# Attention score products issued in pairs, their steps spread over fewer gate units, and three loads re-cut, in a two-layer hybrid trunk on one core

## The chip, the cores and the metric

One Trainium2 chip, one of its cores. The metric is the device time of one execution in microseconds, the median over repeated executions of the same program.

## The reference

Two trunk layers (L0 and L1 here) run over 256 context tokens and 256 latent tokens of width 1024, all in fp32. Layer 0 treats both streams; layer 1 needs the context only as keys, values and state, so that 256 tokens pass through most of it. For each layer, cut to what matters:

```
h      = rmsnorm(x) * (1 + scale) + shift            # modulation from ada_w, 1024 x 6144
q,k,v,u,g = split(h @ w_in)                          # g: 2 x 1024 gate columns
p      = softmax(q0 k0^T) - lam * softmax(q1 k1^T)   # two maps per head, 4 heads, 64 wide each
o      = rmsnorm(p @ v) * (1 - lam_init)
y      = S5(u)       # two directions, 32 groups of 16 channels, 64 states, by chunks of 8 tokens
ps     = glu(gelu(y)) @ w_br_s ;  pa = o @ w_br_a
x     += gate1 * rmsnorm((sigmoid(ga)*pa + sigmoid(gs)*ps) @ w_out)
x     += gate2 * rmsnorm(relu(h2 @ w1 + b1)^2 @ w2 + b2)
```

## The kernel before, in words

Every large product is made of three TensorE matmuls: weights and activations are each split into a rounded part and a rest (`mm3`, lines 159 to 161). The weights come as 114 units per layer of 128x1024 floats (512 KB). `unit` hands them out in a fixed order; `prefetch` allots a tile of the pool `raw` (five tiles), issues the load from SP's queue, and ScalarE (`whi`, line 153) and VectorE (`wlo`, line 155) split it.

A layer runs: the four `u` units, the keys (`k`, 4 units), the queries (`q`, 4), the values (`v`, 4 token tiles), then a loop of **16 gate units** `j` (tiles named `ga`), then the readout of the state space (`y`), the branch products (`pa`, `glu`, `psb`), the output product (`mo`) with a `tail`, and the MLP (`m1p`, `m2p`). Work that fills in is kept in generators which these stages step:

- `attn` yields once for each of its items (16 heads-by-tile in L0, 8 in L1, and one more step to finish). An item is `att1` (two score products `S` at line 917, their row maximum on VectorE at line 918, their exponential `p` on ScalarE at line 920), then one step later `att2` (transposes `pdt`, line 932, and four products `o` with the values, line 936) and, after a tile's last head, `att3`. `AV` steps it among the values, `AJ` says over how many gate units the rest is spread. A score product has 64 rows: map 0 uses rows 0 to 63, map 1 rows 64 to 127. Each fp32 product is shown in the trace as two matmuls. The banks come from `bbank`, of which there are two (`PAB[1]`).
- `ada_gen(L, g)` makes a part of the modulation: eight loads of 512 KB into `raw` tiles, eight matmuls (four products, line 299) for each load, and a last step with the sums. It yields after each load's matmuls. `pump` steps the first generator of a common list `bgq`; `PK`, `PV`, `PG`, `PY` and `PB` say how often in each stage.
- `scan` steps the state, `ssm_in` and `ssm_out` prepare its matrices; `ssm_out` writes, for each of four chunks of eight groups, `CL` to DRAM (`cl`) and a small kernel table `kt` to DRAM (`kd`).

`ygen` does the readout. For each bank it adds three products per group: with `M` (a shifted copy of the kernel table, read from `kd` by an access that overlaps itself, in runs of 128 floats), and two with `CLs`/`CLl` (the `cl` tables). In the kernel before, `ygen` itself issues the loads: two `M` tiles of 1 MB, then the `cl` tables, some in tiles of the pool `x` (`xtile`, three tiles of 512 KB, called `CLl`), the others in slots of the big pool `act` (15 slots of 1 MB, called `CLs`). `s2copy` (at gate unit `SJ`) ends scan and attention and copies the states into `S2`.

The order in which the instructions stand on each engine and on SP's queue is fixed when the program is built, by a planner with its own costs (`schedule_with_timeline_sim`): it takes the instructions in the program's order of priority, but may put a later one ahead when its operands and its tile are free. On the chip, each engine and SP's queue work strictly in the order so fixed.

Of the kernel before, what the change touches and what calls it, by code (L numbers as in the profile page):

```python
# [36 lines left out]
MAGIC = 12582912.0  # L37
HP = 0
TL = True
AJ = [14, 16]  # L40
SJ = [15, 10]
PM = [2, 0, 0, 6]
AK = 6
# [25 lines left out]
YA = [15, 15]  # L69
YN = [2, 1]  # L70
UA = {2: 1, 3: 3}
NX = [4, 2]
LW = [1, 0]
HFA = [(3,), (0, 1, 2, 3), (), (1, 2, 3)]
HFQ = [(), (0, 1, 2, 3)]
# [10 lines left out]
def trunk(tc, I, out):  # L86
    nc = tc.nc
    ctx = ExitStack()
    with ctx:
# [30 lines left out]
        def slot(shape, dt=F32, name="a"):  # L120
            return shaped(act.tile([128, 2048], dt, name=name, tag="a"), shape)
# [20 lines left out]
            return ap.bitcast(F32)  # L142

        nosync = mybir.DependencyInfo(mybir.DependencyClass.NoSync, mybir.DependencyReason.DATA)
        hold = {}

        def after(op, prev):
# [131 lines left out]
        def ada_gen(L, g):  # L279


            c0, n = (0, 512) if g == 0 else (1024 + 1024 * g, 256)
            ncb = n // 128
            ps = pd_.tile([128, 512], F32, name="ada")
            for k in range(8):
                rows = I["ada_w"][L, k * 128:(k + 1) * 128]
                if (L, g) == (0, 0) and k < AK:
                    full = slot([2, 1024], name="adaw")
                    S.dma_start(out=full.rearrange("p j c -> p (j c)"), in_=rows[:, 0:2048])
                    raws = [full[:, 0], full[:, 1]]  # L290
                else:
                    raws = []
                    for jp in range(n // 256):
                        raw = rawp.tile([128, 1024], F32, name="raw", tag="raw")
                        S.dma_start(out=raw, in_=rows[:, c0 + jp * 1024:c0 + (jp + 1) * 1024])
                        raws.append(raw)
                for j in range(4):
                    raw, o = raws[j * n // 1024], j * n % 1024
                    PE.matmul(ps[32 * j:32 * j + 32, :n], cs[:, k, :], raw[:, o:o + n], start=(k == 0), stop=(k == 7))  # L299
                yield  # L300
            R = m2(n, name="row")
            if g in (1, 4):
                ab, gr = m2(n, name="ab"), m2(n, name="gr")
                S.dma_start(out=ab, in_=I["adab"][L, :, g // 4])
                S.dma_start(out=gr, in_=I["grow"][L, :, g // 4])
                V.tensor_tensor(R, ps[:, :n], ab, op=OP.add)
                V.tensor_tensor(R, R, gr, op=OP.mult)
                dd = dram.tile([2, 1024], F32, name=f"ggd{L}_{g}")
                for j in range(4):
                    S.dma_start(out=dd[:, j * n:(j + 1) * n], in_=R[32 * j:32 * j + 2])  # L310
                ggd[L, g] = dd
            else:
                A.activation(R[:, 0:n // 2], ps[:, 0:n // 2], AF.Copy)
                V.tensor_copy(R[:, n // 2:n], ps[:, n // 2:n])
                for cb in range(ncb):
                    PE.transpose(ps[:, cb * 128:(cb + 1) * 128], R[:, cb * 128:(cb + 1) * 128], ident)
                mt = perl.tile([128, 4, ncb, 2], F32, name=f"mod{g}")
                ptv = ps[:, :n].rearrange("p (cb j w) -> p j cb w", cb=ncb, j=4)[:, :, :, 0:2]

                def col(o, nj):  # L320
                    return vecs[L][:, o:o + ncb * nj].rearrange("p (j c) -> p j c", j=nj)[
                        :, :, :, None].to_broadcast([128, nj, ncb, 2])
                V.tensor_tensor(mt, ptv, col({0: V_AB, 2: V_SH2, 3: V_SC2}[g], 4), op=OP.add)
                if g == 0:
                    V.scalar_tensor_tensor(mt[:, 2:4], mt[:, 2:4], 1.0, col(V_G0, 2), op0=OP.add, op1=OP.mult)
                elif g == 3:
                    V.scalar_tensor_tensor(mt, mt, 1.0, col(V_G2, 4), op0=OP.add, op1=OP.mult)
                mods[L, g] = mt.rearrange("p j cb v -> p (j cb) v")
            yield
# [11 lines left out]
        def ssm_params(L):  # L341
# [123 lines left out]
            ssmt[L]["b2"] = pcs[:, 640:1696].rearrange("p (r g h) -> p r g h", r=2, g=33)  # L465
            ssmt[L]["et"] = [dram.tile([128, 8, 2, 128], F32, name=f"et{L}_{c}") for c in range(4)]
            ssmt[L]["cl"] = [dram.tile([128, 8, 2, 128], F32, name=f"cl{L}_{c}") for c in range(4)]
            ssmt[L]["kd"] = [dram.tile([16, 16, 240], F32, name=f"kd{L}_{h}") for h in range(2)]
            yield

        def ssm_b(L):
# [58 lines left out]
        def ssm_out(L, c):  # L530
# [24 lines left out]
                                       op0=OP.mult, op1=OP.add)  # L555
            V.tensor_copy(kt[:, :, 128:240], pf[:, :, 16:128])
            for j in range(4):
                o = 8 * (c % 2) + j
                S.dma_start(out=z["kd"][c // 2][:, o:o + 5:4], in_=kt[32 * j:32 * j + 16])
            z["done", c] = True  # L560
            yield

# [201 lines left out]
        for L in range(DEPTH):  # L764
# [144 lines left out]
            def att1(t, nk, h):  # L909
                qc = (t - t0) * 128  # L910
                mx = small.tile([128, 2], F32, name="mx", tag="mx")
                lsum = small.tile([128, 2], F32, name="lsum", tag="lsum")
                pp = []
                for m in range(2):
                    ps = bbank("S")
                    rr = slice(64 * m, 64 * m + 64)
                    PE.matmul(ps[:, :nk], qT[rr, h, qc:qc + 128], kT[rr, h, 0:nk], start=True, stop=True)  # L917
                    V.tensor_reduce(mx[:, m:m + 1], ps[:, :nk], axis=AX.X, op=OP.max, negate=True)
                    p = m2(nk, name="p")
                    A.activation(p, ps[:, :nk], AF.Exp, bias=mx[:, m:m + 1], accum_out=lsum[:, m:m + 1])  # L920
                    pp.append(p)
                V.reciprocal(lsum, lsum)
                V.tensor_tensor(lsum[:, 1:2], lsum[:, 1:2], nlam, op=OP.mult)
                A.activation(pp[0], pp[0], AF.Copy, scale=lsum[:, 0:1])
                V.scalar_tensor_tensor(pp[0], pp[1], lsum[:, 1:2], pp[0], op0=OP.mult, op1=OP.add)
                return pp[0]

            def att2(t, nk, h, p, po):
# [4 lines left out]
                pd = m2(nk, name="pdT")  # L933
                A.activation(pd, pt[:, :nk], AF.Copy)
                for j in range(nkt):
                    PE.matmul(po[:, h * 128:(h + 1) * 128], pd[:, j * 128:(j + 1) * 128],
                              Vk[:, j, h * 128:(h + 1) * 128], start=(j == 0), stop=(j == nkt - 1))

            def att3(t, po):
                qc = (t - t0) * 128  # L940
# [90 lines left out]


            ysb, yg, ygh, ygl = [], [], [], []

            def ygen():
                ysb.append(slot([4 // A_, 8, 2, 64], name="ysb"))
                Ms = {}
                while ("done", 3) not in z:
                    pump()
                for gh in range(2):  # L1040
                    M = slot([16, 128], name="M")
                    kd = z["kd"][gh]
                    S.dma_start(out=M.rearrange("p g n -> p (g n)"),
                                in_=bass.AP(tensor=kd.tensor, offset=kd.offset, ap=[[16, 8], [240, 256], [1, 128]]))
                    Ms[gh] = M
                CLs = {}
                for qd in range(8):
                    if qd < NX[L]:
                        t = xtile("CLl").rearrange("p (g r n) -> p g r n", g=4, r=2)
                        S.dma_start(out=t, in_=z["cl"][qd // 2][:, qd % 2 * 4:qd % 2 * 4 + 4])  # L1050
                        CLs[qd] = t
                    elif qd % 2 or qd == NX[L]:
                        if qd % 2 == 0:
                            t = slot([8, 2, 128], name="CLs")
                            S.dma_start(out=t, in_=z["cl"][qd // 2])
                            CLs[qd], CLs[qd + 1] = t[:, 0:4], t[:, 4:8]
                        elif qd not in CLs:
                            t = slot([4, 2, 128], name="CLs")
                            S.dma_start(out=t, in_=z["cl"][qd // 2][:, 4:8])
                            CLs[qd] = t  # L1060
                    elif qd not in CLs:
                        t = slot([8, 2, 128], name="CLs")
                        S.dma_start(out=t, in_=z["cl"][qd // 2])
                        CLs[qd], CLs[qd + 1] = t[:, 0:4], t[:, 4:8]
                for b in range(8 // A_):
                    ps = bbank("y")
                    for gi, r, a in np.ndindex(4, 3, A_):
                        g = b * 4 * A_ + 4 * a + gi
                        if r == 0:
                            w, mv = U[:, g, 64 - ncol:64], Ms[g // 16][:, g % 16]  # L1070
                        else:
                            w, mv = S2[g // 16][:, g % 16, r - 1], CLs[g // 4][:, g % 4, r - 1]
                        PE.matmul(ps[ncol * a:ncol * a + ncol, gi * 128:gi * 128 + 128], w, mv,
                                  start=(r == 0), stop=(r == 2), tile_position=(0, ncol * a))
                    A.activation(ysb[0][:, b // 2, :, b % 2].rearrange("p t (g h) -> p g t h", g=4),
# [34 lines left out]
            for j in range(16):  # L1110
# [3 lines left out]
                step(at, -(-nitem * (j + 1) // AJ[L]) - -(-nitem * j // AJ[L]))  # L1114
                step(sc, 8)
                pump(PG[L][j // 4])
                if j == SJ[L]:
                    s2copy()
                if j >= YA[L]:
# [311 lines left out]
```

## Time and profile before

| | us |
|---|---|
| median of three runs | 1327.86 (1326.23 to 1328.57) |
| the profiled execution, its time | 1329.41 |
| its span in the profile | 1327.3 |
| TensorE matmul busy | 1236.9 (93%) |
| VectorE, ScalarE, GpSimd busy | 876.1, 535.1, 239.8 |
| TensorE idle, 1327.3 less 1236.9 | 90.4 |
| mean granted TensorE clock | 0.977 |

Lines such as L917 are lines of the kernel before. A matmul's printed duration includes some time in which the next one already runs; what it costs the engine is the distance from its start to the next start. Half a clock (PEclk 0.50) is 1.2 GHz, a whole one 2.4 GHz.

### The profile page before, as it was taken

How to read it: one execution, taken by the hardware profiler on the slowest of the kernel's cores; microseconds unless marked ns; L12 is line 12 of the kernel's file. 1: busy time of each engine (PE TensorE's matmuls, PEld its weight loads, DVE VectorE, ACT ScalarE, POOL GpSimd, SP SyncE). 2: the span in 40 equal slices, each digit the busy share in tenths (PEclk: the TensorE clock that was granted, in tenths of full speed). 3: DMA queues.
4: the chain of work that ended last, by engine and by line, in shares of the span. 5: the costliest groups of instructions: out<-in, count | busy, mean ns of one | idle time of the engine just before them, and what ended most of it. 6: DMA issues, size and time to landing. Idle time of an engine off the chain costs nothing.

```text
span 1327.3 us, 20706 instructions
## 1 busy us (share of the span) xinstructions
PE 1236.9 (93%) x8032; PEld 1000.1 (75%) x8032; DVE 876.1 (66%) x1786; ACT 535.1 (40%) x929; POOL 239.8 (18%) x284
## 2 busy tenths in 40 slices
PE   4699999997899999999999999989998889899997
PEld 1697767665777796677887888878776778799996
DVE  8779744433376764589978656844676757776666
ACT  1643345445343541222322223533453544544442
POOL 0001088500000330101201112611000001213122
PEclk9799999998999999999999999999999889999999
DMA  9353452216536355832454534368345786466562
GB/s 370 140 156 131 151 195 84 96 56 165 216 113 236 122 183 181 285 113 92 155 185 149 166 113 168 136 197 304 151 152 125 304 278 222 159 192 189 185 186 91
DMA packets 77043, 228.62 MB, mean 172 GB/s; under 512 B 15985, under 2 KB 26897, under 8 KB 72977
## 3 DMA queue, kind: packets, MB, share of 16 engines
q1 hardware_dynamic: 68624, 225.21, 50.5%
q10 hardware_dynamic: 8320, 2.10, 0.7%
q8 instruction: 63, 1.03, 0.3%
q14 instruction: 36, 0.29, 0.1%
HBM read 205.29 MB, written 21.99 MB: 171 GB/s over the span
## 4 chain that ended last, share of the span: by engine, by line
PE 77%; DVE 12%; DMA 5%; ACT 3%; issue 2%; POOL 1%; SPq 1%; DVEq 0%; ACTq 0%; POOLq 0%
PE m1p L159 6%; PE m1p L161 6%; PE m1p L160 6%; PE m2p L159 5%; PE m2p L160 5%; PE m2p L161 5%; PE ga L159 3%; PE ga L160 3%; PE ga L161 3%; PE ada L299 3%; PE S L917 3%; PE mo L159 2%; PE mo L160 2%; PE mo L161 2%; DMA raw<-in_wts 2%
## 5 line engine op out<-in xcount | busy, mean ns | idle before, releaser
L153 ACT ACTIVATE whi<-raw 128x1024 fp32r<-128x1024 f32 x208 | 219.6, 1060 | 381.0 <-PE m2p L161 97.1
L155 DVE TENSOR_TENSOR wlo<-raw,whi 128x1024 fp32r<-128x1024 f32 x200 | 248.0, 1242 | 127.8 <-ACT whi L153 125.3
L1252 POOL TENSOR_TENSOR zz<-zz 128x512 f32<-128x512 f32 (+1 forms) x64 | 88.7, 1386 | 414.9 <-ACT hid L1251 409.2
L159 PE MATMUL m1p<-h,whi 128*128 128x512 f32 (+1 forms) x448 | 151.7, 339 | 0.0
L161 PE MATMUL m1p<-h,wlo 128*128 128x512 f32 (+1 forms) x448 | 150.9, 337 | 0.0
L160 PE MATMUL m1p<-l,whi 128*128 128x512 f32 (+1 forms) x448 | 150.6, 336 | 0.0
L159 PE MATMUL m2p<-whi,hid 128*128 128x512 f32 x288 | 113.7, 395 | 0.2 <-DVE acc L1290 0.2
L160 PE MATMUL m2p<-wlo,hid 128*128 128x512 f32 x288 | 112.5, 391 | 0.0
L161 PE MATMUL m2p<-whi,hid 128*128 128x512 f32 x288 | 112.3, 390 | 0.0
L159 PEld LDWEIGHTS m1p<-h,whi 128*128 128x128 f32 x448 | 84.9, 189 | 13.1 <-issue 3.8
L160 PEld LDWEIGHTS m1p<-l,whi 128*128 128x128 f32 x448 | 84.9, 189 | 9.0
L161 PEld LDWEIGHTS m1p<-h,wlo 128*128 128x128 f32 x448 | 84.9, 189 | 9.0 <-issue 0.2
L159 PE MATMUL ga<-hh,whi 128*128 128x512 f32 (+1 forms) x256 | 89.4, 349 | 1.7 <-ACT whi L153 1.7
L161 PE MATMUL ga<-hh,wlo 128*128 128x512 f32 (+1 forms) x256 | 88.7, 346 | 0.0
L160 PE MATMUL ga<-hl,whi 128*128 128x512 f32 (+1 forms) x256 | 88.0, 344 | 0.0
L299 PE MATMUL ada<-raw,cs 128*32 128x256 f32 (+1 forms) x592 | 55.3, 422 | 13.7 <-DMA raw<-in_ada_w 13.7
L159 PEld LDWEIGHTS m2p<-whi,hid 128*128 128x128 f32 x288 | 54.0, 188 | 15.4 <-issue 2.5
L160 PEld LDWEIGHTS m2p<-wlo,hid 128*128 128x128 f32 x288 | 54.1, 188 | 12.4 <-issue 1.9
L161 PEld LDWEIGHTS m2p<-whi,hid 128*128 128x128 f32 x288 | 54.1, 188 | 11.0
L159 PEld LDWEIGHTS ga<-hh,whi 128*128 128x128 f32 x256 | 48.9, 191 | 15.4 <-issue 8.7
L1253 DVE TENSOR_TENSOR hid<-zz,hid 128x512 fp32r<-128x512 f32 (+1 forms) x64 | 37.9, 595 | 27.8 <-POOL zz L1252 27.5
L161 PEld LDWEIGHTS ga<-hh,wlo 128*128 128x128 f32 x256 | 49.0, 191 | 9.3 <-issue 4.1
(309 smaller groups left out, 2859.9 us busy)
## 6 DMA issues: line engine op xcount, KB each, us to landing
raw<-in_wts SPq DMA_DIRECT2D x227, 512.0 KB, 4.3
raw<-in_ada_w SPq DMA_DIRECT2D x84, 512.0 KB, 6.1
cl<-CL SPq DMA_DIRECT2D x8, 1024.0 KB
adaw<-in_ada_w SPq DMA_DIRECT2D x6, 1024.0 KB, 11.6
CLs<-cl SPq DMA_DIRECT2D x5, 1024.0 KB
x<-in_x SPq DMA_DIRECT2D x8, 512.0 KB, 4.6
M<-kd SPq DMA_DIRECT2D x4, 1024.0 KB
et<-ET SPq DMA_DIRECT2D x4, 1024.0 KB
```

The lines of the kernel that those rows point to most:

```text
L153: a = A.activation(hi, src, AF.Copy)
L155: eng.tensor_tensor(lo, src, f(hi), op=OP.subtract)
L159: after(PE.matmul(ps, sh, mh, start=first, stop=False), prev)
L160: PE.matmul(ps, sh, ml, start=False, stop=False)
L161: PE.matmul(ps, sl, mh, start=False, stop=last)
L299: PE.matmul(ps[32 * j:32 * j + 32, :n], cs[:, k, :], raw[:, o:o + n], start=(k == 0), stop=(k == 7))
L917: PE.matmul(ps[:, :nk], qT[rr, h, qc:qc + 128], kT[rr, h, 0:nk], start=True, stop=True)
L1252: G.tensor_tensor(zz, zz, zz, op=OP.mult)
L1253: V.tensor_tensor(lo, zz, f(hi), op=OP.subtract)
```

## The change

It does five things. The two score products of a head are issued one after the other, with a wait of the first for the exponential of the head before (so that both banks are free) and behind the last `o` product of the head before that. The rest of the attention items is spread over 12 gate units in L0 (14 before) and 13 in L1 (16 before). `ada_gen` yields after every second load (for all but its first part), so that a step does two. The kernel table `kd` is cut in four by chunk, and `M` in four tiles of 512 KB, three of which are loaded into `x` tiles from within the gate loop (units 11, 12, 13 in L0 and 0, 4, 8 in L1) and the fourth inside `ygen`. The `cl` tables then all go to `act` slots, one for each chunk.

```diff
-AJ = [14, 16]
+AJ = [12, 13]
...
-NX = [4, 2]
+MJ = [(11, 12, 13), (0, 4, 8)]
...
@@ ada_gen
-                yield
+                if g == 0 or k % 2:
+                    yield
...
-            ssmt[L]["kd"] = [dram.tile([16, 16, 240], F32, name=f"kd{L}_{h}") for h in range(2)]
+            ssmt[L]["kd"] = [dram.tile([16, 8, 240], F32, name=f"kd{L}_{c}") for c in range(4)]
...
@@ att1
-                pp = []
+                pp, pss = [], []
                 for m in range(2):
                     ps = bbank("S")
                     rr = slice(64 * m, 64 * m + 64)
-                    PE.matmul(ps[:, :nk], qT[rr, h, qc:qc + 128], kT[rr, h, 0:nk], start=True, stop=True)
+                    o = PE.matmul(ps[:, :nk], qT[rr, h, qc:qc + 128], kT[rr, h, 0:nk], start=True, stop=True)
+                    if m == 0 and "exp" in hold:
+                        tc.add_manual_dep(o.ins, hold["exp"].ins.name, sync, reason="both banks")
+                        after(o, hold.get("o"))
+                    pss.append(ps)
+                for m, ps in enumerate(pss):
                     V.tensor_reduce(mx[:, m:m + 1], ps[:, :nk], axis=AX.X, op=OP.max, negate=True)
                     p = m2(nk, name="p")
-                    A.activation(p, ps[:, :nk], AF.Exp, bias=mx[:, m:m + 1], accum_out=lsum[:, m:m + 1])
+                    hold["exp"] = A.activation(p, ps[:, :nk], AF.Exp, bias=mx[:, m:m + 1], accum_out=lsum[:, m:m + 1])
...
+            def mload():
+                while ("done", 3) not in z:
+                    pump()
+                q = len(Ms)
+                M = (slot([1024], name="M") if q == 3 and last else xtile("M"))
+                kd = z["kd"][q]
+                S.dma_start(out=M, in_=bass.AP(tensor=kd.tensor, offset=kd.offset, ap=[[16, 8], [240, 128], [1, 128]]))
+                Ms.append(M.rearrange("p (g n) -> p g n", g=8))
...
@@ ygen
-                for gh in range(2):
-                    M = slot([16, 128], name="M")
-                    kd = z["kd"][gh]
-                    S.dma_start(out=M.rearrange("p g n -> p (g n)"),
-                                in_=bass.AP(tensor=kd.tensor, offset=kd.offset, ap=[[16, 8], [240, 256], [1, 128]]))
-                    Ms[gh] = M
...
+                while len(Ms) < 3:
+                    mload()
+                CLs = []
+                for c in range(4):
+                    CLs.append(slot([8, 2, 128], name="CLs"))
+                    S.dma_start(out=CLs[c], in_=z["cl"][c])
+                    if c == 1 and last:
+                        mload()
                 for b in range(8 // A_):
+                    if b == 1 and not last:
+                        mload()
...
@@ the loop of gate units
+                if j in MJ[L]:
+                    mload()
```

## Rows read from the trace of the kernel before

**Rows 1.** The page, busy time by engine and the chain that ended last.

```profile
PE 1236.9 (93%) x8032; PEld 1000.1 (75%) x8032; DVE 876.1 (66%) x1786; ACT 535.1 (40%) x929; POOL 239.8 (18%) x284
...
PE 77%; DVE 12%; DMA 5%; ACT 3%; issue 2%; POOL 1%; SPq 1%; DVEq 0%; ACTq 0%; POOLq 0%
```

**Rows 2.** Waits of PE (waiter, waited for: us in total, times, longest).

```profile
PE ada L299 <- DMA raw<-in_ada_w: 13.7, 8, 9.5
...
PE y L1073 <- DMA M<-kd: 6.3, 1, 6.3
...
PE y L1073 <- ACT on L949: 3.6, 1, 3.6
...
PE S L917 <- ACT p L920: 2.1, 3, 1.0
```

**Rows 3.** Windows, score products alone: length, busy (count), PEclk, DMA share, GB/s.

```profile
150.00:225.00 75.00, 7.25 (x32) 0.98 0.49 165
225.00:305.00 80.00, 16.39 (x32) 1.00 0.24 76
940.00:1022.00 82.00, 16.84 (x32) 1.00 0.38 108
```

**Rows 4.** Timeline of PE among the gates: start, us, line, operands, count.

```profile
222.21 0.70 PE L917 MATMUL S<-kT,qT 64*128 64x256 f32 x4
...
227.39 1.13 PE L917 MATMUL S<-kT,qT 64*128 64x512 f32 x4
...
256.52 0.39 PE L161 MATMUL ga<-hh,wlo 128*128 128x512 f32 x1
256.84 1.12 PE L917 MATMUL S<-kT,qT 64*128 64x512 f32 x2
257.89 0.50 PE L159 MATMUL ga<-hh,whi 128*128 128x512 f32 x1
```

**Rows 5.** Windows, all engines: length, busy (count), PEclk, DMA share, GB/s.

```profile
322.00:327.50 5.50, 5.50 (x43) 5.17 (x44) 0.00 (x0) 0.00 (x0) 0.00 (x0) 0.50 0.69 125
...
334.30:337.70 3.40, 2.96 (x28) 2.96 (x30) 0.00 (x0) 0.00 (x0) 0.00 (x0) 0.50 0.99 410
...
1010.00:1023.00 13.00, 13.00 (x114) 9.68 (x112) 8.20 (x32) 4.25 (x12) 0.00 (x0) 1.00 0.61 127
...
1032.60:1037.40 4.80, 4.74 (x29) 3.27 (x30) 4.48 (x12) 4.11 (x7) 0.00 (x0) 0.50 1.04 429
...
887.00:930.00 43.00, 43.00 (x341) 35.10 (x341) 18.02 (x35) 15.40 (x22) 5.52 (x6) 1.00 0.85 298
```

**Rows 6.** Timeline of SP's queue at the two readouts.

```profile
309.29 7.46 SPq L1043 DMA_DIRECT2D M<-kd  x2
...
1007.60 7.83 SPq L1043 DMA_DIRECT2D M<-kd  x2
1016.22 7.80 SPq L204 DMA_DIRECT2D raw<-in_wts  x1
1024.11 0.38 SPq L295 DMA_DIRECT2D raw<-in_ada_w  x1
```

**Rows 7.** Timeline of PE, modulation products among the keys of L1.

```profile
893.23 0.64 PE L299 MATMUL ada<-raw,cs 128*32 128x256 f32 x8
...
899.47 1.50 PE L299 MATMUL ada<-raw,cs 128*32 128x256 f32 x24
```

**Rows 8.** Timeline of SP's queue ahead of L1.

```profile
853.82 0.32 SPq L1050 DMA_DIRECT2D CLl<-cl  x1
854.23 4.12 SPq L204 DMA_DIRECT2D raw<-in_wts  x4
```

**Rows 9.** Timeline of DVE and ACT behind the score product of 258.55.

```profile
259.74 0.68 DVE L918 TENSOR_REDUCE mx<-S 128x1 f32<-128x512 f32 x1
...
261.04 0.19 ACT L920 ACTIVATION_READ_ACCUMULATOR p<-S,mx 128x1 f32 x1
```

**Rows 10.** Windows, modulation products alone, as in rows 3.

```profile
1007.00:1090.00 83.00, 10.03 (x128) 0.90 0.80 260
```

More of the change, by code (lines that the diff above doesn't have):

```diff
@@ L144, in trunk @@
         nosync = mybir.DependencyInfo(mybir.DependencyClass.NoSync, mybir.DependencyReason.DATA)
+        sync = mybir.DependencyInfo(mybir.DependencyClass.Sync, mybir.DependencyReason.DATA)
         hold = {}
@@ L557, in ssm_out @@
             for j in range(4):
-                o = 8 * (c % 2) + j
-                S.dma_start(out=z["kd"][c // 2][:, o:o + 5:4], in_=kt[32 * j:32 * j + 16])
+                S.dma_start(out=z["kd"][c][:, j:j + 5:4], in_=kt[32 * j:32 * j + 16])
             z["done", c] = True
@@ L935, in att2 @@
                 for j in range(nkt):
-                    PE.matmul(po[:, h * 128:(h + 1) * 128], pd[:, j * 128:(j + 1) * 128],
-                              Vk[:, j, h * 128:(h + 1) * 128], start=(j == 0), stop=(j == nkt - 1))
+                    hold["o"] = PE.matmul(po[:, h * 128:(h + 1) * 128], pd[:, j * 128:(j + 1) * 128],
+                                          Vk[:, j, h * 128:(h + 1) * 128], start=(j == 0), stop=(j == nkt - 1))
             def att3(t, po):
@@ L1033, in trunk @@
             ysb, yg, ygh, ygl = [], [], [], []
+            Ms = []
+            def mload():
[6 more added lines that the diff above has]
+                Ms.append(M.rearrange("p (g n) -> p g n", g=8))
             def ygen():
@@ L1036, in ygen @@
                 ysb.append(slot([4 // A_, 8, 2, 64], name="ysb"))
-                Ms = {}
-                while ("done", 3) not in z:
-                    pump()
-                for gh in range(2):
-                    M = slot([16, 128], name="M")
-                    kd = z["kd"][gh]
-                    S.dma_start(out=M.rearrange("p g n -> p (g n)"),
-                                in_=bass.AP(tensor=kd.tensor, offset=kd.offset, ap=[[16, 8], [240, 256], [1, 128]]))
-                    Ms[gh] = M
@@ L1046, in ygen @@
[L1046 to L1064, printed above, removed]
+                while len(Ms) < 3:
+                    mload()
@@ L1069, in ygen @@
                         if r == 0:
-                            w, mv = U[:, g, 64 - ncol:64], Ms[g // 16][:, g % 16]
+                            w, mv = U[:, g, 64 - ncol:64], Ms[g // 8][:, g % 8]
                         else:
-                            w, mv = S2[g // 16][:, g % 16, r - 1], CLs[g // 4][:, g % 4, r - 1]
+                            w, mv = S2[g // 16][:, g % 16, r - 1], CLs[g // 8][:, g % 8, r - 1]
                         PE.matmul(ps[ncol * a:ncol * a + ncol, gi * 128:gi * 128 + 128], w, mv,
```

## The prediction

> **What bounds it now.** The page comes first: TensorE is busy for 1236.9 of 1327.3 us, and it holds 77% of the chain that ended last [rows 1]. So a matmul made cheaper counts at once wherever TensorE has no gap, and a transfer counts only where TensorE stands still for it. Next I read who keeps TensorE waiting [rows 2]. Of its 90 us of idle time, three waits touch this change: 6.3 us of the readout products for `M`, 3.6 us for ScalarE's `on` behind them in the same readout of L0, and 9.5 us, the longest of those for modulation loads. SP's queue says where that one comes from [rows 6]: at 1007.60 it issues L1's two `M` loads, 7.83 us long; the next weight load takes another 7.80 us to go out; and the modulation load behind it goes at 1024.11. The windows show why [rows 5]: between 1010 and 1023 the DMA engines moved 127 GB/s, just behind it 429 GB/s. In L0 it is the same: `M` goes out at 309.29, and in 322 to 327.5 the transfers run at 125 GB/s. `M` is read in runs of 128 floats (512 bytes), weights in rows of 4 KB. After each stall the granted clock is 0.50, that is 1.2 GHz, for some microseconds: TensorE is busy for 5.5 and 2.96 us at half a clock in L0, and for 4.74 us in L1 [rows 5].
>
> Last come the score products. Alone, one of 512 columns takes 1.05 us: its start is 256.84, the next matmul's 257.89 [rows 4]. Where the two of a head happen to stand together (x4), both are over in 1.13 us: they use different halves of the rows and run side by side. With 256 columns the four take 0.70 us.
>
> **Part by part, against the profiled execution's 1329.4 us.**
>
> *Pairs.* The score products occupy 7.25 us in L0's context heads, 16.39 us in its latent heads and 16.84 us in L1 [rows 3], 32 matmuls, so 8 heads, each. All in pairs they would be 8 x 0.70 = 5.6, 8 x 1.13 = 9.0 and 9.0 us. That saves 1.6 + 7.4 + 7.8 = 16.8 us. The gates around them show no gap, so it is TensorE's time and the path's. The lower bound is half of that, 8 us, if the added wait keeps some pairs from being reached in time. I take 16. The wait itself I cost at nothing: attention items stand about one gate unit apart in L0 (14 items over 12 units) and over two units apart in L1 (5 over 13), and the exponential waited for ends about 2.3 us after a pair (below, third rival). Other work hides it as long as gate matmuls stand in between. Queued behind the waiting product on TensorE is everything, the next gate unit first.
>
> *L0's readout.* With `M` loaded in units 11 to 13, the 6.3 us go, and with attention done by unit 12 the `o` products and `on` no longer stand in the readout: 3.6 us more. Half of the 5.5 + 2.96 us at the low clock, 4.2 us, goes if the gap does. Together 14.1 us, the upper bound. What is late next is the first `cl` table: all four now wait for `act` slots, which come free with the last gate unit, but each is 1 MB at 429 GB/s, 2.4 us, and the first bank needs one only. I take 10; the lower bound is 3, if the tables or `S2` are as late as `M` was.
>
> *L1's readout.* Three quarters of `M` leave the queue there; the last, 512 KB, takes 4.1 us at 127 GB/s and is needed only by the second bank. The modulation loads leave it too: 128 matmuls, 16 loads, run between 1007 and 1090 [rows 10]; at two loads a step, L1's 32 need 20 steps, of which 14 come ahead of the gates, so that they are over by gate unit 5. The 9.5 us and half of 4.74 us at the low clock go: 11.9 us, the upper bound. I take 10, and 4 as the lower bound.
>
> *Longer runs.* Eight modulation matmuls take 0.64 us, 24 in a run 1.50 us [rows 7], so each further load costs 0.43, and a load that joins a run saves 0.21 us. Of 64 loads in the parts affected at most 32 join: 6.7 us. Since runs of 24 exist already, I take 3; the lower bound is 0.
>
> *What the new places cost.* Each `M` tile keeps the DMA engines for 4.1 us (512 KB at 127 GB/s), where the `cl` tile that had its `x` tile took 1.2 us (at 429). The planner puts such loads ahead: the `cl` tile for L1's readout went out at 853.82, 170 us early, ahead of four weight loads of L1's first products [rows 8]. If `M` takes that place, those weights come 2.9 us later each time, and at worst three tiles in a row delay them by 3 x 4.1 less 2 x 1.2, 9.9 us; if the loads stay in the gates, where the DMA share is 0.38 [rows 3], nothing. And the modulation loads that leave L1's readout go to its keys: by the end of the keys 24 loads are done where it was 13 (two steps of the tail and 12 among the keys, one of 14 being a last step). Eleven more at 1.2 us are 13.4 us of transfers, and between 887 and 930 the engines are busy for 0.85 already: 6.5 us are free, 7 us are not. From 0 to 23 us in all; I take 4 for the weights and 4 for the keys, because the queries and values behind the keys step no modulation and can take up most of it.
>
> Here the Trainium skill would say otherwise. Its page "DMA: Bandwidth & Descriptors", Specifications, gives 512 B as the smallest transfer that still runs at line rate. By that rule an `M` tile would cost 1.2 us like any other, and the 4 us for the weights would be 0, the forecast 4 us lower; the trace shows 512-byte runs at 127 GB/s against 429, so I go by the rows.
>
> *Nothing else moves the sum.* `kd` in four tiles makes the same 32 small writes. `act` slots asked for in the readout stay the same in number, four in L0 (2 + 2, now 4) and five in L1 (2 + 3, now 4 + 1). Earlier attention is the same instructions on all engines; ScalarE, which it leans on, has room (535 us busy).
>
> Sum: 16 + 10 + 10 + 3 - 8 = 31 us, so 1298.4 us for an execution like the profiled one. That one was 1.5 us above the median of the runs, so **1297 us**. All upper bounds give 16.8 + 14.1 + 11.9 + 6.7 = 49.5 us less, 1278; all lower bounds 8 + 3 + 4 - 23 = 8 us more, 1336.
>
> **Rivals.**
>
> *First: the stall in the readouts changes its name.* `M` arrives early, but the readout then waits for `cl` tables or `S2`, since the slots come free no sooner. For it: four 1 MB tables, all in slots, where up to four half-tables had `x` tiles. Against: finishing attention gives back the slots of keys, queries and values. The readouts then give 3 + 4 us instead of 20, and the longer runs nothing: 1297 + 16 = 1313 us.
>
> *Second: the keys of L1 and the start of the layers become DMA-bound.* Price 23 us in place of 8: 1312 us. For it: the share of 0.85; against: TensorE had no gap there (43.00 of 43.00 us) and the planner can place modulation later.
>
> *Third, slower: the pair waits for both banks.* Behind the product that started at 258.55 and ended at 259.61, its reduction starts at 259.74 and its exponential's sum ends at 261.23 [rows 9], 1.6 us; in a pair the second reduction stands behind the first, 0.7 us more, so the next pair can start 2.3 us after this one. Were TensorE to stand there at each of 24 heads, that is 55 us: 1352 us. It turns the result from 31 / 24 = 1.3 us a head on. Against it: in the trace the 48 products, each free to go with one bank, wait for an exponential 2.1 us in all [rows 2], and where heads follow at a distance the wait has long been met. This is the rule of the Trainium skill's page "TensorEngine Tiling (Array Packing)", PSUM Bottleneck: tiling makes the matmuls faster, not the evacuation of PSUM, which may then bind. The trace bears out its half: 1.13 us for a pair against 2.3 us until its banks are free.
>
> *Fourth: nothing much happens.* The planner had paired the context heads almost wholly (7.25 against 5.6 us), and if it also keeps loads and runs where they were, the rest nets out near 1327.
>
> **Chances.** Forecast 0.59 (its own range 1281 to 1309), first rival 0.20, second 0.10, third 0.07, fourth 0.04. The range for 8 in 10 goes from 1281 to 1322: up to there it takes in the first two rivals. About 0.2% (2.7 us) is what a measurement of this kernel can tell from no change. Faster by more: 0.87, the first three cases with a little taken off for several of their lower bounds at once; within it: 0.05; slower: 0.08.
>
> **What would show it.** Score products all as x4 with 1.1 us, about 24 us busy in all in place of 40; no wait of `y` for `M`; SP's queue without a 7 us issue at the readouts; the 0.50 clock windows near 322, 334 and 1030 gone; no wait for a modulation load above 2 us after 1000. The forecast is wrong if TensorE waits for `p` before pairs for more than 10 us in all, if `y` waits for `cl`, or if gaps appear among L1's first products and keys.

## The result and the profile after

The changed kernel takes 1312.4 us (median of 4 runs, 1309.7 to 1313.4), the kernel before on the same chip 1327.8 us: a ratio of 0.9892, 95% interval 0.9871 to 0.9914. By the ratio that is 14.3 us faster (0.0108 x 1327.8); 31 were forecast. The profiled execution took 1312.2 us.

The page after, the same two lines as [rows 1]:

```profile
PE 1221.8 (93%) x8032; PEld 999.0 (76%) x8032; DVE 874.9 (67%) x1786; ACT 531.4 (41%) x929; POOL 248.7 (19%) x284
...
PE 77%; DVE 12%; DMA 5%; ACT 3%; issue 2%; POOL 1%; SPq 0%; DVEq 0%; ACTq 0%; POOLq 0%
```

TensorE works 15.1 us less than before, but its idle time is as it was: 1310.4 - 1221.8 = 88.6 us, where it had been 90.4. Both stalls of the readouts were to go, so others have come. Its waits after, which answer to [rows 2]:

```profile
PE ada L300 <- DMA raw<-in_ada_w: 7.7, 7, 3.8
...
PE u L160 <- ACT whi L154: 6.7, 4, 4.4
PE ot L960 <- ACT on L956: 4.8, 1, 4.8
...
PE y L1073 <- DMA M<-kd: 3.9, 1, 3.9
...
PE glu L160 <- ACT whi L154: 3.4, 1, 3.4
```

The wait for `M` has shrunk from 6.3 to 3.9 us, the longest wait for a modulation load from 9.5 to 3.8. The wait for `on` has gone from L0's readout and stands in L1's attention; those of `u` and `glu` are waits for weights, which ScalarE splits into `whi` as they land. No score product waits for `p`.

The score products alone, in the windows of [rows 3]:

```profile
150.00:225.00 75.00, 6.14 (x32) 0.95 0.55 185
225.00:305.00 80.00, 9.54 (x32) 0.97 0.28 97
940.00:1022.00 82.00, 7.90 (x28) 0.94 0.43 148
```

They take 6.1, 9.5 and (28 of 32 in that stretch) 7.9 us, close to the 5.6, 9.0 and 9.0 of the forecast: 25.8 us in all, down from 40.5.

SP's queue at the two readouts, as in [rows 6]:

```profile
308.85 6.66 SPq L1060 DMA_DIRECT2D CLs<-cl  x4
315.83 0.64 SPq L1050 DMA_DIRECT2D M<-kd  x1
320.05 14.84 SPq L606 DMA_DIRECT2D x<-in_x  x3
338.34 0.33 SPq L296 DMA_DIRECT2D raw<-in_ada_w  x1
...
339.23 4.59 SPq L296 DMA_DIRECT2D raw<-in_ada_w  x4
...
346.51 13.56 SPq L296 DMA_DIRECT2D raw<-in_ada_w  x4
360.18 9.49 SPq L205 DMA_DIRECT2D raw<-in_wts  x6
...
1027.20 1.07 SPq L1050 DMA_DIRECT2D M<-kd  x1
```

`M` no longer blocks the queue. But nine modulation loads go out from 338.34 on, the last four of them taking 13.56 us, and six weight loads stand behind them until 360.18. The windows show what that does, as in [rows 5]:

```profile
300.90:307.70 6.80, 6.26 (x20) 3.83 (x17) 3.48 (x7) 4.95 (x8) 0.00 (x0) 0.50 0.01 2
320.00:330.00 10.00, 6.11 (x76) 4.98 (x72) 1.84 (x8) 3.56 (x9) 0.00 (x0) 0.91 0.89 250
360.00:371.00 11.00, 4.95 (x43) 3.07 (x36) 6.95 (x10) 5.90 (x8) 0.00 (x0) 0.76 0.87 300
914.00:945.00 31.00, 28.46 (x376) 22.50 (x372) 16.77 (x38) 16.77 (x28) 3.89 (x4) 1.00 0.95 346
997.20:1007.40 10.20, 7.97 (x47) 4.29 (x48) 9.17 (x42) 4.94 (x13) 0.00 (x0) 0.50 0.29 80
```

TensorE stands for 3.9 of 10 us waiting for the fourth `M`, and for 6 of the 11 us from 360 on, first for a modulation load and then for the gated unit's weights. In L1 it stands for 2.5 of 31 us while the DMA engines are busy for 0.95. In the 10.2 us from 997.20 on, which begin within the `on` wait in L1, it is busy for 7.97 us at a granted clock of 0.50 (1.2 GHz).

So L0's downward products (`psb`) start at 387.3 us, 1.4 us later than before, though the forecast had put 19 us of its gain ahead of that point (9 of the pairs, 10 of the readout). Those of L1 start at 1077.5, 17.2 us earlier.

### The profile page after: what moved, and what is told of

Its sections match the earlier page's. It is cut to its first block, busy times and chain, and to the rows that moved or that the text cites. A ratio compares the mean times of both kernels' runs of the same rounds, so it can differ in the third digit from the quotient of the medians.

```text
span 1310.4 us, 20693 instructions
## 1 busy us (share of the span) xinstructions
PE 1221.8 (93%) x8032; PEld 999.0 (76%) x8032; DVE 874.9 (67%) x1786; ACT 531.4 (41%) x929; POOL 248.7 (19%) x284
## 4 chain that ended last, share of the span: by engine, by line
PE 77%; DVE 12%; DMA 5%; ACT 3%; issue 2%; POOL 1%; SPq 0%; DVEq 0%; ACTq 0%; POOLq 0%
PE m1p L160 6%; PE m1p L162 6%; PE m1p L161 6%; PE m2p L160 5%; PE m2p L161 5%; PE m2p L162 5%; PE ga L162 3%; PE ga L160 3%; PE ga L161 3%; PE mo L160 3%; PE mo L161 3%; PE mo L162 3%; PE ada L300 2%; DMA raw<-in_wts 2%; DVE wlo L156 2%
## 5 line engine op out<-in xcount | busy, mean ns | idle before, releaser
L1254 POOL TENSOR_TENSOR zz<-zz 128x512 f32<-128x512 f32 (+1 forms) x64 | 97.1, 1518 | 402.4 <-ACT hid L1253 402.4
L160 PEld LDWEIGHTS m2p<-whi,hid 128*128 128x128 f32 x288 | 54.4, 189 | 16.4 <-DVE acc L1292 2.6
L840 POOL TENSOR_TENSOR sh<-sh,rope 128x256 f32<-128x256 f32 x16 | 18.4, 1150 | 207.9 <-DVE sh L839 195.8
L1292 DVE TENSOR_TENSOR acc<-m2p,acc 128x512 f32<-128x512 f32 x60 | 40.9, 686 | 25.0 <-PE m2p L162 25.0
```

Source lines behind the costliest of these rows:

```text
L160: after(PE.matmul(ps, sh, mh, start=first, stop=False), prev)
L840: G.tensor_tensor(sh, sh, rope[:, 1], op=OP.mult)
L1254: G.tensor_tensor(zz, zz, zz, op=OP.mult)
L1292: V.tensor_tensor(acc(ti, half), ps, bias2[:, half * 512:(half + 1) * 512] if grp == 0 else acc(ti, half), op=OP.add)
```

## The experiments

Fourteen kernels, each timed against the kernel before on its own chip. "Gain" is (1 - ratio) x 1327.8 us.

| kernel | median us | ratio (95% interval) | gain us |
|---|---|---|---|
| changed | 1312.4 | 0.9892 (0.9871 to 0.9914) | 14.3 |
| changed, short runs | 1300.3 | 0.9799 (0.9770 to 0.9828) | 26.7 |
| changed, old loads | 1322.7 | 0.9969 (0.9955 to 0.9983) | 4.1 |
| changed, no pairs | 1313.3 | 0.9896 (0.9861 to 0.9930) | 13.8 |
| changed, `M` pinned | 1322.8 | 0.9968 (0.9951 to 0.9984) | 4.2 |
| before + new loads | 1302.5 | 0.9820 (0.9800 to 0.9839) | 23.9 |
| before + pairs | 1319.1 | 0.9947 (0.9926 to 0.9967) | 7.0 |
| before + longer runs | 1329.4 | 1.0033 (1.0021 to 1.0046) | -4.4 |
| changed, half pace | 1305.4 | 0.9843 (0.9821 to 0.9864) | 20.8 |
| changed, long runs in L0 only | 1304.5 | 0.9854 (0.9829 to 0.9879) | 19.4 |
| changed, half the loads in L0's readout | 1306.1 | 0.9838 (0.9812 to 0.9863) | 21.5 |
| short runs, no pairs | 1304.1 | 0.9834 (0.9816 to 0.9852) | 22.0 |
| short runs, pairs in L1 only | 1297.8 | 0.9801 (0.9778 to 0.9824) | 26.4 |
| short runs, heads over 14 units | 1307.5 | 0.9867 (0.9846 to 0.9887) | 17.7 |
| short runs, heads over 10 units | 1300.7 | 0.9805 (0.9781 to 0.9829) | 25.9 |

A difference between two rows carries some 4 to 5 us (their two half intervals taken together), so the smaller splits below are sizes and not exact shares. The earlier attention steps are the one part that was not run alone. "Short runs, no pairs" is the new loads with these steps and nothing else: 22.0 us, where the new loads alone give 23.9.

### One part of the change undone

**Short runs.** One modulation load a step again:

```
-                if g == 0 or k % 2:
-                    yield
+                yield
```

> The changed kernel with one part undone: the modulation generator yields after every load again, so that a step does one load and not two. Theory A (the missing 15 us went to modulation loads that now stand ahead of weights among L0's values and L1's keys): the gates of L0 start near 179 us again instead of 188, L1's queries and values lose their waits, and the time falls by 8 to 14 us, to 1298 to 1304. Theory B (the early M loads hold the weights back): the late gates stay, the time is within 3 us of 1312 or up to 5 us above, since the merged runs are lost. Theory C (the loss lies in L0's readout): no change of the start of the gates, time 1309 to 1316.

Measured 1300.3 us, 12.3 us less than the changed kernel (0.0093 of 1327.8). That is theory A's time, though L0's gates start at 182.3 us and not near 179. The longer runs, forecast to give 3 us, are its largest loss. By the page TensorE is busy for 1221.3 us, as in the changed kernel, so the difference between the two spans, 13.7 us, is idle time almost wholly: 75.4 us in place of 88.6. Two waits are shorter than in the changed kernel (6.7 and 4.8 us there), and two have no line any more, `y` for `M` (3.9) and `glu` for its weights (3.4):

```profile
PE u L160 <- ACT whi L154: 3.3, 3, 1.8
...
PE ot L959 <- ACT on L955: 0.8, 1, 0.8
```

What the runs were to save is there, only small. The modulation products alone in the changed kernel, and then with short runs:

```profile
166.00:390.00 224.00, 17.96 (x245) 0.95 0.48 166
390.00:880.00 490.00, 14.17 (x110) 0.99 0.45 152
880.00:1080.00 200.00, 18.56 (x224) 0.96 0.66 233
```

```profile
166.00:390.00 224.00, 15.66 (x172) 0.95 0.44 149
390.00:880.00 490.00, 20.23 (x192) 0.99 0.49 164
880.00:1080.00 200.00, 16.41 (x216) 0.97 0.66 237
```

They take 50.7 and 52.3 us (sums of three rows). But two loads a step also ask for them sooner: 245 products, not 172, lie ahead of 390 us. At eight matmuls a load that is 9 more loads of 512 KB by then.

**Old loads.** `M` and the tables are loaded in the readout again, `kd` in two halves:

```
-                if j in MJ[L]:
-                    mload()
...
-            ssmt[L]["kd"] = [dram.tile([16, 8, 240], F32, name=f"kd{L}_{c}") for c in range(4)]
+            ssmt[L]["kd"] = [dram.tile([16, 16, 240], F32, name=f"kd{L}_{h}") for h in range(2)]
```

> The changed kernel with the loads undone: the kernel table in two halves, M and the cl tables loaded inside the readout as before. Pairs, attention steps and longer runs stay. Theory A: the gates of L0 still start near 187 us, and the readouts stall again for M: time 1318 to 1326. Theory B: the gates of L0 start near 180 us and L1's first products lose their wait of 4.4 us, which pays for the readouts: time 1306 to 1314. Theory C (the new loads bring nothing in L0's readout): 1312 to 1318, all of it lost in L1.

Measured 1322.7 us, 10 us more than the changed kernel, within theory A's range. The readout's waits for `M` are back, 11.0 us, with 11.3 us for `on`.

**No pairs.** The score products as before:

```
-                pp, pss = [], []
+                pp = []
...
-                    pss.append(ps)
-                for m, ps in enumerate(pss):
                     V.tensor_reduce(mx[:, m:m + 1], ps[:, :nk], axis=AX.X, op=OP.max, negate=True)
```

> The changed kernel with the pairs undone: each score product is followed by its own reduction and exponential, no added wait. If the pairs are worth what the trace shows in busy time (25.8 us against 40.5), the time rises by 12 to 17 us, to 1324 to 1329, and score products are busy for about 40 us. If their wait costs on the path what they save, the time stays within 3 us of 1312.

Measured 1313.3 us, 0.5 us more by the ratios, though the score products are back at 40.4 us of TensorE's time. Inside the changed kernel the pairs are worth nothing that can be measured. Two of its waits are not there without pairs, though the runs are as long: that for the fourth `M`, and that for `on` in L1 (0.8 us in place of 4.8). So these two take both parts together.

**`M` pinned.** Each load of `M` waits for the tanh of the gate unit in which it is written, so that the planner can't put it ahead of weights:

```
+                if "gate" in hold:
+                    tc.add_manual_dep(d.ins, hold["gate"].ins.name, sync, reason="not ahead of its gate unit")
```

> The changed kernel with one wait added: the M load asked for in a gate unit may not go out before that unit's tanh, so that the planner can't put it 30 to 170 us ahead. Theory B: L0's gates start 4 to 8 us earlier, L1's first products lose their wait (4.4 us and half of the 10 us of low clock behind it): time 1300 to 1306. Theory A: only L1's start gains, 2 to 4 us: 1308 to 1311. Theory C: 1310 to 1314.

Measured 1322.8 us, 10 us more than the changed kernel and above all three ranges, so the loads that went out early were not its loss. Its waits:

```profile
PE y L1075 <- DMA CLs<-cl: 7.3, 1, 7.3
...
PE y L1075 <- DMA M<-kd: 3.3, 2, 2.6
...
PE u L160 <- ACT whi L154: 3.3, 3, 1.9
```

The tables behind `M` in SP's queue now arrive 7.3 us late. `u`'s wait for weights does fall, from 6.7 to 3.3 us, but that does not show the forecast's price for `M` ahead of weights: the wait is 6.4 us with the old loads, where `M` goes out in the readout, and 3.3 with short runs, where it goes out as early as in the changed kernel.

### One part alone

**Before + new loads.** The loads by chunk and in the gates, nothing else (the inverse of the edit above).

> The kernel before with the shifted kernels kept by chunk and loaded in the gates, and nothing else of the change. My sum for the two readouts was 20 us less 4 for the weights; undoing this part in the changed kernel cost 10 us. Theory E, it is worth the same 10 us alone: about 1317 us, the wait of the readout products for the shifted kernels gone but for L0's fourth tile (some 4 us). Rival F, without the earlier end of attention and with modulation still in L1's readout it is worth less than 5 us, since the next late item (the o products, the tables, the modulation loads) takes the wait over: 1322 to 1328 us.

Measured 1302.5 us: this part alone gains 23.9 us, more than the whole change and more than either theory gave it. Its wait for modulation loads, in all, is now:

```profile
PE ada L299 <- DMA raw<-in_ada_w: 3.7, 5, 2.9
```

L0's downward products start 12.6 us earlier than before (373.3), and L1 from its first product to its downward products takes 226.5 us in place of 240.9, 14.4 less. No wait for `M` is left, and the 9.5 us wait for a modulation load is gone too, though modulation goes at its old pace: it was the queue behind `M`.

**Before + pairs.**

> The kernel before with the score products in pairs alone. Theory C, pairs pay where transfers leave room, and before has its modulation at one load a step: 8 to 16 us less, about 1312 to 1319 us against 1327. Rival D, they are worth nothing: 1325 to 1328 us. Third theory: with attention's items over 14 and 16 gate units the wait for both banks costs something: above 1328 us.

Measured 1319.1 us, a gain of 7.0 us (4.4 to 9.8 by the interval): under half of the 16, and just short of theory C's 8. In its trace TensorE works 18.3 us less than before, and L0's downward products start at 377.2 us, 8.7 us earlier. But L0's last heads now wait 3.8, 2.3 and 4.0 us, and the long wait in L1, 9.5 us for a modulation load before, stands there as 9.3 us of `ga` for weights.

**Before + longer runs.**

> The kernel before with the longer runs of modulation alone. My term was 3 us less. Theory G, two loads a step crowd the transfers of that kernel too: 5 to 12 us more, 1332 to 1339 us. Rival, the loss comes only together with the shifted kernels that now share those stretches, and before is the same or up to 7 us faster: 1320 to 1328 us.

Measured 1329.4 us, a loss of 4.4 us (2.8 to 6.1 by the interval), just short of theory G's 5 to 12. The three parts alone add up to 23.9 + 7.0 - 4.4 = 26.5 us; together, with the earlier attention steps, they give 14.3. Of the missing 12 us the longer runs are the larger part, not the whole: without them the other parts give 26.7 us where they add up to 30.9, some 4 us less; with them the kernel loses 12.3 us and not 4.4, some 8 us more.

### Where the longer runs lose

**Half pace.** Runs as long as in the changed kernel, but an empty step behind each:

```
-                if g == 0 or k % 2:
+                if g == 0:
+                    yield
+                elif k % 2:
+                    yield
                     yield
```

> The changed kernel with its runs of modulation matmuls as long as they are (two loads in a step), but after each such step one step that does nothing, so that loads are asked for at the pace of the kernel before. Theory A1, the pace costs: two loads a step crowd the transfers of weights in the keys and values of L1 and in the readout of L0, and it is this that the 12 us of the short runs are; then this kernel comes to about 1300 us, as the short runs did, with the score of L1's queries ending near 912 us. Theory A2, the run itself costs: 24 or more modulation matmuls in one piece hold up TensorE or the buffers behind them whatever the pace; then it stays at about 1312 us.

Measured 1305.4 us: between the two. 6.5 of the 12.3 us (ratio 0.9892 to 0.9843) go with the pace; 5.8 stay with the long run. L1's last query product starts at 914.6 us (942.6 in the changed kernel, 912.3 with short runs), as the pace theory has it; part of that is order, since in the changed kernel the state space's products `V` end before the queries do, and in the other two after them.

**Long runs in L0 only.**

```
-                if g == 0 or k % 2:
+                if L or g == 0 or k % 2:
```

> The changed kernel with two modulation loads a step in L0's modulation alone, one in L1's. From the traces, the 13.8 us between the long and the short runs split into 16 up to L0's downward products, 7 given back in L0's MLP, and some 4 in L1. Theory I, the loss sits in L0's readout, where 16 loads go out in a bunch ahead of the fourth shifted kernel and the gated unit's weights: 1308 to 1310 us, waits of the readout for the fourth tile and for weights as in the changed kernel. Rival, it sits in L1's keys and queries: 1301 to 1303 us.

Measured 1304.5 us: of the 12.3 us, 7.3 belong to L0's modulation (0.9799 to 0.9854) and 5.0 to L1's. That lies between the two expectations: L0's part is the larger by the medians, but not nearly all, and within the noise the two could be equal. In L1's share the wait for `on`, in the changed kernel, is a part that can be seen:

```profile
998.74 1.25 PE L960 MATMUL ot<-ident,on 128*128 128x128 f32 x4 [4.81 <-ACT on L956]
```

With long runs in L0 only it is 0.8 us.

**Half the loads in L0's readout.** Long runs, but a step after every second output block in place of every one:

```
-                    pump(PY[L])
                     if blk % 2:
+                        pump(PY[L])
                         pa_unit(blk // 2)
```

> The changed kernel, longer runs and all, but with two modulation steps in L0's readout in place of four, so eight loads there in place of sixteen; the eight left out of it are done later, in L0's MLP. Theory I, the loads that bunch in the readout ahead of the weights of the gated unit are the loss in L0 (7 of the 12 us): L0's downward products start near 378 in place of 387, and the kernel comes to 1304 to 1307 us, with no wait of the gated unit for its weights. Rival, it is not the number of loads in that place but the heads before it that stand late (the wait for ScalarE at the end of the attention and the fourth shifted kernel): 1310 us or more.

Measured 1306.1 us, 7.2 us less than the changed kernel (0.9892 to 0.9838), with L0's downward products at 378.3. (At eight matmuls and one load for each k, four steps are eight loads and two are four; the sixteen and eight of the expectation were counted double.) SP's queue there:

```profile
339.20 0.33 SPq L296 DMA_DIRECT2D raw<-in_ada_w  x1
...
340.10 0.86 SPq L296 DMA_DIRECT2D raw<-in_ada_w  x2
...
343.97 3.21 SPq L296 DMA_DIRECT2D raw<-in_ada_w  x2
347.45 14.91 SPq L205 DMA_DIRECT2D raw<-in_wts  x6
362.46 6.60 SPq L296 DMA_DIRECT2D raw<-in_ada_w  x4
```

Five modulation loads go out from 339 on ahead of the six weight loads, where it was nine; the next four follow behind them. So the weights go from 347.45 on and not from 360.18, and the wait of `glu` for weights is gone. The wait for the fourth `M` is not (3.7 us). This `M` goes out at 314.80, behind the four tables; but with short runs it goes out later, at 318.87, and nothing waits for it. What differs is the work in between. The modulation products alone, in the changed kernel and then with short runs:

```profile
300.00:329.00 29.00, 0.00 (x0) 0.87 0.60 195
```

```profile
300.00:329.00 29.00, 5.90 (x56) 0.89 0.66 247
```

With half the loads in the readout there are none either. Of the twelve traces with the new loads, four have none there and wait long for this `M` (the changed kernel, this one, long runs in L0 only, heads over 10 units): 2.8 to 3.9 us. In the six with 48 to 64 such products there is no such wait. The rows fit an account in which the background products also filled TensorE's time while `M` came, and the longer runs had used them up. No run changes this alone, and the two others, also without such products, fit less well: `M` pinned waits 0.7 us, behind the late tables, and the changed kernel without pairs not at all.

### Where the pairs' time goes

**Short runs, no pairs.**

> The changed kernel with one modulation load a step and with the score products as they were before (each after the other's evacuation). Theory C, the 15 us of TensorE's time that pairs save are swallowed by the transfers that the longer runs crowd, so that without the longer runs they come through: about 1312 us, that is 10 to 14 us above the 1300.3 of the short runs with pairs. Rival D, pairs are worth nothing in this kernel since the score products stood in TensorE's time that something else would have left idle: about 1301 us.

Measured 1304.1 us: without the long runs the pairs give 4.6 us (0.9834 to 0.9799), not 10 to 14. In these two traces L0's downward products start at the same 371.2 us, and L1's at 1071.4 without pairs, 1063.8 with: L1 gets its 7.6 us, L0 nothing. (That is one execution of each; the spans of these two lie 7.6 us apart, the kernels by the ratios 4.6.) The windows at the end of L0's attention, with pairs, then without:

```profile
290.00:300.00 10.00, 6.94 (x28) 4.27 (x28) 4.05 (x9) 4.98 (x13) 0.00 (x0) 0.64 0.04 13
300.00:310.00 10.00, 9.46 (x38) 6.24 (x37) 5.47 (x14) 8.25 (x13) 0.00 (x0) 0.67 0.16 42
```

```profile
290.00:300.00 10.00, 10.00 (x50) 8.36 (x49) 3.73 (x6) 5.17 (x12) 0.00 (x0) 1.00 0.33 107
300.00:310.00 10.00, 9.94 (x53) 6.58 (x52) 6.96 (x17) 7.53 (x14) 0.00 (x0) 1.00 0.08 26
```

In the same 20 us TensorE issues 66 products with pairs and 103 without, at a granted clock of about 0.65 and 1.00. The timeline of PE with pairs says why:

```profile
291.37 1.16 PE L942 MATMUL o<-Vk,pdT 128*128 128x128 f32 x8 [2.17 <-ACT pdT L940]
292.45 1.72 PE L917 MATMUL S<-kT,qT 64*128 64x512 f32 x4
294.10 1.11 PE L938 MATMUL pdt<-ident,p 128*128 128x128 f32 x4
296.91 2.08 PE L942 MATMUL o<-Vk,pdT 128*128 128x128 f32 x8 [1.69 <-ACT pdT L940]
```

The last heads follow each other with no gate product between, so TensorE waits for the chain through VectorE and ScalarE (2.17, then 1.69 us), and behind the first wait the clock falls: at half clock the same eight `o` products take 2.08 us in place of 1.16. What ScalarE does in the first wait:

```profile
289.39 0.68 ACT L926 ACTIVATE p<-S,mx 128x512 f32<-128x512 f32 x1
...
290.05 0.69 ACT L926 ACTIVATE p<-S,mx 128x512 f32<-128x512 f32 x1
...
290.71 0.60 ACT L940 ACTIVATE pdT<-pdt 128x512 f32<-128x512 f32 x1
```

It empties both score banks of the next head with their exponentials before it copies the transposes that the `o` products wait for. The Trainium skill's page "TensorEngine Tiling (Array Packing)", section PSUM Bottleneck, says that tiling quickens the matmuls and not what empties PSUM (the memory in which matmuls leave their results). The rows agree, for L0's last heads alone.

**Short runs, pairs in L1 only.** `att1` takes the new form `if last:` and the old one otherwise.

> The changed kernel with one modulation load a step, and with pairs in L1 alone; L0's score products as before. In the traces of the two short-run kernels, with pairs and without, L0's downward products start at the same 371.2 us, while L1's are 7.6 us apart. Theory H, L0's saving of about 9 us is lost within L0, to the last heads that stand together without gate work between them (waits of 2.17 and 1.69 us and 13.7 us at a granted clock of 0.5): the same time as with pairs in both, about 1300 us. Rival, pairs in L0 still give something that the trace of one execution hides: 1303 us or more.

Measured 1297.8 us, a ratio of 0.9801 where pairs in both layers have 0.9799. L0's pairs are worth nothing here, and in this trace the two waits and the low clock near 300 us are gone. Its median is the lowest of all, but by their intervals it can't be told from short runs with pairs in both layers, from heads over 10 units (0.9805, below), or even from the kernel before with the new loads alone (0.9820).

**Short runs, heads over 14 units, and over 10.**

```
-AJ = [12, 13]
+AJ = [14, 13]
```

> The changed kernel with one modulation load a step and L0's heads over 14 gate units in place of 12. By theory H the heads of L0 that end the attention stand without gate work between them; spread over more units the waits of about 4 us and the stretch at the low clock (13.7 us, so 6.8 us of work lost) shrink, and the kernel comes to 1292 to 1296 us. Rival: the planner places the heads by when their inputs and buffers are ready and not by the unit they are issued in, so that the bunch stays or moves into the readout: 1299 us or more.

> The changed kernel with one modulation load a step and L0's heads over 10 gate units in place of 12. Over 14 units the time was some 9 us longer, with waits of the last heads of 3.8, 2.3 and 4.0 us. Theory J, pairs end a head's attention in a chain of DVE and ScalarE that needs gate units behind it, so earlier still is better: the waits near 290 and the stretch at the low clock go, and L0 gives its part of the pairs: 1293 to 1297 us. Rival, the heads are held by VectorE and by the buffers of the scores and not by the unit they are issued in, or the heads among fewer units bring waits of their own: 1299 us or more.

Measured 1307.5 us over 14 units, 9 us worse than over 12; 1300.7 over 10, the same. The remedy fell both times. Over 14 units the chain's waits are longer:

```profile
PE ot L959 <- ACT on L955: 4.6, 2, 3.8
...
PE pdt L938 <- DVE p L931: 4.0, 1, 4.0
```

These are the waits that the kernel before with pairs has too, and its heads also go over 14 units. So in L0 pairs need the earlier heads: over 14 units this kernel gains 17.7 us, less than the new loads alone (23.9). Over 10 the waits of 2.17 and 1.69 us stand where they stood, at 289.7 and 295.7 us. So the place of L0's last heads isn't set by the unit in which they are issued once it is early enough. What sets it stays open; no run here can tell.

## Why the prediction was wrong in size

The direction held, and the time lies in the range of 1281 to 1322 us, though not in the forecast's own (1281 to 1309); the forecast of 31 us was twice the gain.

- **The steps that failed are "Longer runs" and "Pairs".** Taken in the order new loads with earlier heads, pairs, longer runs, the table gives 22.0 + 4.6 - 12.3 = 14.3 us. The forecast, with its 4 us for the keys counted to the runs, whose new pace they price, is 16 + 16 - 1 = 31. Pairs and longer runs each fell short by 11 us, and 6 us more from the loads hid part of that. Taken with the pairs last, the longer runs cost 8.2 us and the pairs give 0.5; their sum is the same.
- **Longer runs** were costed on the wrong side. I costed them as TensorE's time: 0 to 6.7 us saved, 3 taken; their pace I priced for L1's keys alone. That time did fall, by some 1.6 us. The cost lay where I hadn't looked: two loads a step move modulation ahead, 9 more loads before 390 us, into a readout that already has to bring tables, `M` and weights. Undone, it gives 12.3 us. Half the steps in L0's readout give back 7.2 us, which shows the bunch there to be one cause; half the pace everywhere gives 6.5. How much of the rest is products that no longer fill the readout stays open. I had used the loads' new pace as an argument for L1's readout; the new loads alone show that it wasn't needed there.
- **Pairs** were mis-sized: 16 taken, 8 the lower bound, 7.0 measured alone, 4.6 with short runs, 0.5 in the changed kernel. The cost of the products came out as worked out (25.8 us for 24), and no pair waited for its banks. I had costed the wait at nothing "as long as gate matmuls stand in between"; between L0's last heads none stand. "The gates around them show no gap, so it is TensorE's time and the path's" holds in L1 in the two traces with short runs, where 7.6 of the forecast 7.8 us are seen, and not in L0 there, where what was saved came back as waits between the last heads and a low clock behind them. In the trace of the kernel before with pairs, L0's downward products did come 8.7 us forward, so it is not L0 as such.
- **The two readouts and the new places** came out better than forecast: 10 + 10 less 4 for the weights is 16 us, measured alone 23.9 (12.6 and 14.4 us in the two layers, less 3.2 elsewhere in the trace). Their upper bounds, 14.1 + 11.9, were the right reading. Of the 4 us for weights behind an early `M`, 2.2 at most are seen: `u` waits 1.0 us for weights before and 3.2 with the new loads alone. The 6.7 of the changed kernel go with the longer runs (6.3 with these alone, where `M` is late). Taking `M` out of its early place costs 10 us. In L0 I named the first table as late next; it is the fourth `M`, 3.9 us. I read the 125 and 127 GB/s as the price of runs of 512 bytes, but [rows 5] give the DMA engines a busy share of only 0.69 and 0.61 there, against 0.99 and 1.04 at 410 and 429 GB/s: in part they stood idle, and no run changes the length of the runs.
- **First rival** (1313 us): the right number for another reason. `y` waits 0.5 us for tables; the stalls did take new names, `on`, `glu` and the fourth `M`, but mostly through the longer runs. **Second rival** (1312 us): L1's queries have their share of 0.95 and 2.5 us of gaps, but L1's modulation is some 5 us of the loss, not all. **Third rival**: no pair waits for an exponential in the trace, though its chain does bind for L0's last heads. **Fourth**: the parts do move the time, one by one.

Of the signs I named, pairs at x4, a short issue of `M` at the readouts and no long wait for modulation after 1000 came true. No wait for `M`, and no low clock in the readouts, did not. Of the signs that it would be wrong, one came true: gaps among L1's first products (`u` waits 6.0 us for weights there).

## What to carry to other kernels

A longer run of a background job is not only fewer switches: it is also more loads asked for per step. Count what the new pace moves into the tightest stretch of the transfer queue, and price it by the loads that stand behind it, before counting TensorE's savings. Look also at what it moves out: background matmuls may be what covers a late transfer. And cheaper matmuls pay where other matmuls stand behind them; where a chain through other engines ends a stage, the saving turns into a wait. Try each part alone before adding the parts up: here one of them alone gives 23.9 of the 26.7 us that any kernel reached.

## What the runs showed that I had not expected

The low clock behind small waits cost more than the waits. With pairs and short runs, TensorE was idle for 3.6 of the 20 us at the end of L0's attention, and the 16.4 us in which it worked ran at a mean granted clock of about 0.65, which by estimate is another 5.7 us of full speed (0.35 x 16.4): together 9.3 us, about the 9 that pairs were to save in L0. And three edits that lose little or gain alone (+23.9, +7.0, -4.4 us) together gave 12 us less than their sum.
